# Second MLP product of a hybrid encoder block on one Trainium2 core: its on-chip buffers laid over other buffers of the first product, the residual in two halves, seven stores issued from GpSimd

## The chip, the cores and the metric

The kernel runs on one core of a Trainium2 chip. The metric is the device time of one execution in microseconds; 1725.57 us is the median of three runs of the kernel before, which lay between 1724.66 and 1726.45 us. TensorE (PE), VectorE (DVE), ScalarE (ACT), GpSimd (POOL) and SyncE (SP) each work through an instruction list of their own, in order, and wait for each other on semaphores. An instruction that waits holds up everything behind it on its engine. Transfers are issued by SP, ACT or POOL and then run on 16 DMA engines.

## The reference, cut to what matters

One layer of an encoder block on 1024 tokens of width 1024, in float32. The change lies in the last line.

```python
def hybrid_layer(x, ...):
    h = rmsnorm(x, norm_mix_w)
    proj = h @ w_in
    ...                                   # SSD mixer and neighbourhood attention
    x = x + jnp.concatenate([y_ssm, y_na], axis=-1) @ w_out
    h = rmsnorm(x, norm_mlp_w)
    return x + jnp.square(jax.nn.relu(h @ w_mlp_in)) @ w_mlp_out   # 1024 -> 4096 -> 1024
```

## The kernel before, in words

**Arithmetic.** A float32 product is made of three matmuls on split factors: every factor is cut into a high part and a remainder, and `chain` adds high x high, high x low and low x high. For the second MLP product, the cut costs an ACT pass (`wh` or the high half of `ahl`, line 759) and a subtraction (line 760), which DVE does for activations (the low half of `ahl`) and POOL for weights (`wl`). Both MLP products also use a scheme of seven block products in the place of eight, always in the order `ORD` = 1, 2, 6, 5, 7, 3, 4; its factors are sums and differences of quarter blocks.

**First MLP product** (class `Block`, eight blocks `fb` of 512 hidden columns). The turned and split activations are the factors `hc[1]` to `hc[7]`, two tiles of 8 KB per partition for each, which stay on chip for all eight blocks. They are called h1 to h7 below. One of its seven products is 24 matmuls. `sums` gathers the results of a block in the tiles `cq`: c11 is complete after product 2, c22 after 7, c12 after 3, c21 after 4. ACT squares them, DVE forms the sums s1, s2, s4 and a difference (lines 1203 to 1211), and `store` writes all seven to DRAM as `act_dr`, from the SP queue.

**Second MLP product** (four blocks `fb`, each over 1024 hidden rows as two halves `u`). One of its seven products is 48 matmuls. Its activations come back from `act_dr` into `ar` (line 1272) and are split into `ahl`. Its weight quarters 11, 21, 12 and 22 (line 1289, tiles `wraw`) are split as they are for 1, 2 and 7, and give t1 = 12 - 11, t2 = 22 - t1, 22 - 12 and 21 - t2 on DVE (lines 1306 to 1310) for the others. `acc` is the residual, loaded from `x2_dr`; the block products are added to it from PSUM (line 1330). The last block stores it to the output.

**What lies where.** The pools of the second product are opened after the first has ended, in the same memory. A tile that covers an old one may not be written before the last reader of the old one is done. In the kernel before, counted along the right-hand side, `acc` (32 KB) covers h6 and h5, the split weights `wy` cover raw weights of the first product, the four `ar` buffers cover h4, and the split activations a1, a3, a2 and the raw weights `ra` cover h7, h3, h2 and h1. Eight raw weight buffers `rb` lie on the left, over the four `cq` tiles. `ORD` ends with product 4, so h4 is the last factor to be read.

**What sets the order.** The order of the instructions on each engine is fixed when the program is built, by a scheduler that models times; a wait that is met earlier or later on the chip does not change it. `tc.issue_after` holds an instruction behind another.

Of the kernel before, what the change touches and what calls it, by code (L numbers as in the profile page):

```python
# [9 lines left out]
F32 = mybir.dt.float32  # L10
# [8 lines left out]
P = 128  # L19
T = 1024  # L20
D = 1024
NT = T // P
# [33 lines left out]
def hymba_block(  # L56
# [1039 lines left out]
    with ExitStack() as ph:  # L1096
# [13 lines left out]
        class Block:  # L1110
# [62 lines left out]
                self.s = sA[:, 0], sA[:, 1], sB[:, 0]  # L1173

            def store(self, i, src):
                nc.sync.dma_start(
                    act_dr[self.fb // 2][i - 1, :, 2 * (self.fb % 2) : 2 * (self.fb % 2) + 2, :],
                    src,
                )
# [68 lines left out]
    with ExitStack() as ph:  # L1248
        phase["ps"] = ph.enter_context(
            tc.tile_pool(name="ps4", bufs=1, space=PSUM, reuse_waits="tile")  # L1250
        )
        xa, wy, ar_, a1, a3, a2, ra = (
            ph.enter_context(tc.tile_pool(name=n, bufs=1, side="right", reuse_waits="tile"))
            for n in ("xa", "wy", "ar", "a1", "a3", "a2", "ra")
        )
        rb = ph.enter_context(tc.tile_pool(name="rb", bufs=1, reuse_waits="tile"))
        acc = xa.tile([P, NT, D], F32, name="acc")
        hls[:] = [wy] * 3 + [wp] * 3
        ring["hl"] = ring["raw"] = 0
        raw_a = [wp] * 2 + [ra] * 4  # L1260
# [9 lines left out]
        def a_split(fb, i, u):  # L1270
            ar = ar_.tile([P, 1024], F32, tag="ar", name="ar", bufs=4)
            nc.sync.dma_start(
                ar.rearrange("p (a t) -> p a t", a=2), act_dr[fb][i - 1, :, 2 * u : 2 * u + 2, :]
            )
            pool = ahl[ring["ahl"] % 6]
            ring["ahl"] += 1
            t = pool.tile([P, 2, 1024], F32R, tag="ahl", name="ahl", bufs=2)
            split_to((t[:, 0], t[:, 1]), ar, nc.vector)
            return t[:, 0], t[:, 1]

        for fb in range(4):
            bq = []
            for u in range(2):
                bq.append({n: raw_of(n) for n in ("11", "21", "12", "22")})
            for n in ("11", "21", "12", "22"):
                for u in range(2):
                    r0 = (2 * fb + u) * 512 + (int(n[0]) - 1) * 256
                    d0 = (int(n[1]) - 1) * 512
                    nc.sync.dma_start(
                        bq[u][n].rearrange("p (a d) -> p a d", a=2),  # L1290
                        w_mlp_out[0][r0 : r0 + 256, d0 : d0 + 512].rearrange(
                            "(a p) d -> p a d", p=P
                        ),
                    )
            X = [ps_mm("px2") for _ in range(4)]
            Y = [ps_tp("py2"), ps_tp("py2"), ps_s("py2"), ps_s("py2")]
            if fb == 0:
                for t in range(NT):
                    nc.sync.dma_start(acc[:, t, :], x2_dr[t])
            for i in ORD:  # L1300
                wa = []
                for u in range(2):
                    q = bq[u]
                    if i == 6:
                        q["t1"], q["t2"] = raw_of("t1"), raw_of("t2")
                        nc.vector.tensor_tensor(q["t1"], q["12"], q["11"], op=sub)
                        nc.vector.tensor_tensor(q["t2"], q["22"], q["t1"], op=sub)
                        nc.vector.tensor_tensor(q["12"], q["22"], q["12"], op=sub)
                    elif i == 4:
                        nc.vector.tensor_tensor(q["21"], q["21"], q["t2"], op=sub)  # L1310
                    src = q[{1: "11", 2: "21", 3: "22", 4: "21", 5: "t1", 6: "t2", 7: "12"}[i]]
                    wa.append((a_split(fb, i, u), w_split(src, nc.gpsimd)))
                if i == 5:
                    Y = [ps_tp("pz2"), ps_tp("pz2"), ps_s("pz2"), ps_s("pz2")]
                for t in range(4):
                    pt = (X if i in (1, 6, 7, 4) else Y)[t]
                    ts = slice(t * P, t * P + P)
                    for u in range(2):
                        (ah, al), (wh, wl) = wa[u]
                        for a in range(2):  # L1320
# [8 lines left out]
                    d = acc[:, tt, dh * 512 : (dh + 1) * 512]  # L1329
                    nc.vector.tensor_tensor(d, d, pt, op=add)  # L1330
# [46 lines left out]
```

## Time and profile before

| | |
|---|---|
| median of 3 runs | 1725.57 us |
| the profiled execution's own time | 1725.33 us |
| its span in the trace | 1723.5 us |
| busy, PE / DVE / ACT / POOL | 1636.0 / 1106.3 / 726.5 / 705.6 us |
| last matmul of the first MLP product ends | 1389.7 us |
| first matmul of the second MLP product | 1399.64 us |
| last matmul of the program | 1719.33 us |

The profile gives 1.8 us less for the span than the execution took. A row of the timeline shows the start, the duration, the engine, the source line, the operation, the tile written and the tile read, with the number of instructions that were merged; in brackets stand the idle time of the engine ahead of it and what ended it. PE busy is 95% of the span, yet the few waits that PE has late in the program stand in its row of waits, and the granted clock is listed for each stretch.

### The profile page before, as it was taken

Reading aid. Unit: us, or ns where it says so; the run is one execution under the profiler, and the core shown is the slowest. Engines: PE = TensorE matmul, PEld = TensorE weight load, DVE = VectorE, ACT = ScalarE, POOL = GpSimd, SP = SyncE. Lnnn points to the kernel's source line nnn. Section 1 sums busy time; section 2 is a strip of 40 time slices with the busy share of each in tenths; the row PEclk is TensorE's granted clock in tenths of the full one; section 3 lists DMA queues with packets and bytes.
Section 4 is the critical chain, followed back from the end, with each engine's and each line's share of the span. In section 5 each row is a group of like instructions: output and inputs, shape, how many; then the busy total and the mean of one; then the engine's idle time right before and its main releaser. Section 6 shows DMA issues by size and latency. Waiting matters only on the chain. (4 is left out here: it accounts for less than half of the span.)

```text
span 1723.5 us, 20879 instructions
## 1 busy us (share of the span) xinstructions
PE 1636.0 (95%) x7461; PEld 1304.6 (76%) x7461; DVE 1106.3 (64%) x1687; ACT 726.5 (42%) x1189; POOL 705.6 (41%) x496
## 2 busy tenths in 40 slices
PE   6999999989888999999999988999999978999999
PEld 5788888777766777777767767788888866888887
DVE  5767214889787744778787776454343359787863
ACT  5434223434344434555565533454444443333330
POOL 4000004888778741221242242244444426555551
PEclk9999999999998999999999999999999989999999
DMA  8213338876675796754453141254344394644231
GB/s 200 62 37 104 89 98 242 210 195 207 213 206 161 234 311 199 240 150 138 132 183 123 56 159 49 73 190 153 134 159 147 125 349 149 201 141 166 92 110 73
DMA packets 178499, 269.75 MB, mean 157 GB/s; under 512 B 13963, under 2 KB 105051, under 8 KB 178395
## 3 DMA queue, kind: packets, MB, share of 16 engines
q1 hardware_dynamic: 135419, 231.18, 42.6%
q10 hardware_dynamic: 42976, 37.23, 7.1%
q8 instruction: 59, 0.97, 0.2%
q14 instruction: 45, 0.37, 0.1%
HBM read 185.21 MB, written 86.50 MB: 158 GB/s over the span
## 5 line engine op out<-in xcount | busy, mean ns | idle before, releaser
L760 POOL TENSOR_TENSOR wl<-wraw,wh 128x1024 fp32r<-128x1024 f32 x110 | 300.1, 2740 | 350.1 <-ACT wh L759 336.7
L745 PE MATMUL px<-wh,ahl 128*128 128x512 f32 x512 | 163.7, 397 | 9.8 <-ACT ahl L759 9.8
L759 ACT ACTIVATE wh<-wraw 128x1024 fp32r<-128x1024 f32 x110 | 115.7, 1054 | 127.4 <-issue 42.4
L179 PE MATMUL pq<-wl,hTh 128*128 128x512 f32 x384 | 153.1, 400 | 4.6 <-DVE wl L149 4.4
L745 PE MATMUL px<-h,wh 128*128 128x512 f32 x496 | 156.5, 396 | 0.0
L178 PE MATMUL pq<-wh,hTh 128*128 128x512 f32 x384 | 153.1, 401 | 1.9 <-ACT wh L148 1.2
L180 PE MATMUL pq<-wh,hTl 128*128 128x512 f32 x384 | 151.9, 396 | 0.0
L759 ACT ACTIVATE ahl<-ar 128x1024 fp32r<-128x1024 f32 x56 | 58.9, 1053 | 173.0 <-PE px L745 89.6
L760 DVE TENSOR_TENSOR ahl<-ar,ahl 128x1024 fp32r<-128x1024 f32 x56 | 107.3, 1917 | 37.4 <-ACT ahl L759 36.2
L745 PEld LDWEIGHTS px<-wh,ahl 128*128 128x128 f32 x512 | 97.3, 190 | 31.9 <-ACT ahl L759 10.2
L745 PEld LDWEIGHTS px<-h,wh 128*128 128x128 f32 x496 | 93.4, 189 | 22.4
L149 DVE TENSOR_TENSOR wl<-wraw,wh 128x1024 fp32r<-128x1024 f32 x40 | 55.0, 1376 | 83.3 <-ACT wh L148 82.7
L878 POOL TENSOR_TENSOR mb<-braw,nam 128x256 f32<-128x256 f32 (+1 forms) x48 | 41.0, 884 | 159.7 <-DVE nmx L936 123.4
L184 ACT ACTIVATE pth<-ptp 128x384 fp32r<-128x384 f32 (+1 forms) x128 | 58.4, 459 | 107.8 <-PE ptp L959 106.8
L745 PE MATMUL px<-wl,ahl 128*128 128x512 f32 x256 | 100.9, 394 | 0.0
L745 PE MATMUL px<-h,wl 128*128 128x512 f32 x248 | 98.1, 396 | 0.0
L179 PEld LDWEIGHTS pq<-wl,hTh 128*128 128x128 f32 x384 | 73.2, 191 | 22.1 <-DVE wl L149 7.9
L149 POOL TENSOR_TENSOR wl<-wraw,wh 128x1024 fp32r<-128x1024 f32 x18 | 43.8, 2446 | 110.5 <-ACT wh L148 84.3
L745 PE MATMUL pz<-wh,ahl 128*128 128x512 f32 x256 | 82.8, 400 | 6.5 <-DVE acc L1330 5.0
L178 PEld LDWEIGHTS pq<-wh,hTh 128*128 128x128 f32 x384 | 72.9, 190 | 18.2 <-ACT wh L148 2.5
L180 PEld LDWEIGHTS pq<-wh,hTl 128*128 128x128 f32 x384 | 73.2, 191 | 14.7
L612 POOL TENSOR_TENSOR rb<-rb,c 128x512 f32<-128x512 f32 x64 | 75.0, 1192 | 21.5 <-DMA rb<-cum_dr 18.7
(265 smaller groups left out, 4242.6 us busy)
## 6 DMA issues: line engine op xcount, KB each, us to landing
act_dr<-cq SPq DMA_DIRECT2D x56, 512.0 KB, 3.0
ar<-act_dr SPq DMA_DIRECT2D x56, 512.0 KB, 3.8
wraw<-in_w_in_dram SPq DMA_DIRECT2D x44, 512.0 KB, 4.0
rb<-cum_dr SPq DMA_DIRECT2D x32, 512.0 KB, 7.6
wraw<-in_w_mlp_in_dram SPq DMA_DIRECT2D x32, 512.0 KB, 4.7
wraw<-in_w_mlp_out_dram SPq DMA_DIRECT2D x32, 512.0 KB, 5.3
q_dr<-hl ACTq DMA_DIRECT2D x64, 128.0 KB, 3.2
k_dr<-hl ACTq DMA_DIRECT2D x16, 512.0 KB, 3.2
```

Of the source, the lines that this page charges most:

```text
L149: lo_eng.tensor_tensor(lo[:, 0:n], raw[:, 0:n], hi[:, 0:n].bitcast(F32), op=sub)
L178: nc.tensor.matmul(pt, lhsT=ah, rhs=bh, start=first, stop=False)
L179: nc.tensor.matmul(pt, lhsT=ah, rhs=bl, start=False, stop=False)
L180: return nc.tensor.matmul(pt, lhsT=al, rhs=bh, start=False, stop=last)
L184: nc.scalar.activation(hi, src, AF.Copy)
L612: nc.gpsimd.tensor_tensor(rb[:, d], rb[:, d], c1[:, d, c, h0 : h0 + 4].unsqueeze(2).broadcast_to([P, 4, P]), op=sub,)
L745: nc.tensor.matmul(pt, lhsT=a, rhs=b, start=f, stop=l, skip_group_check=True)
L759: nc.scalar.activation(hl[0], src, AF.Copy)
L760: eng.tensor_tensor(hl[1], src, hl[0].bitcast(F32), op=sub)
L878: nc.gpsimd.tensor_tensor(mb[:, s].rearrange("p (s r c) -> p s r c", r=16, c=8), v[:, a:b], nam[:, s].rearrange("p (s r c) -> p s r c", r= ...
```

## The change

1. **Pools.** On the right, from the outer end: `rb` (raw weights 12, 22, t1, t2) over h6 and h5, `wy` as before, x0 (the first half of the residual) over h4, `ra` over h7, a2 over h3, a1 over h2, `ar` over h1. On the left, x1 (the second half of the residual) lies over the `cq` tiles of c21, c22 and s4, and a3 over those of c11, c12, s1 and s2. The rings of the pools keep their sizes.
2. **Residual.** `acc` is two tiles of 16 KB, loaded in the first block behind the factors of product 1 and of product 6. In block 1, `issue_after` holds the raw weights behind the second half's load.
3. **Loads of activations** are taken out of `a_split`; those of products 1 and 2 are issued with the raw weights.
4. **22 - 12** is formed for product 7 in the place of product 6, and in the source both halves' quarters are allocated quarter by quarter.
5. **Stores** of the last block of the first product go out from POOL.

```diff
             def store(self, i, src):
-                nc.sync.dma_start(
+                (nc.gpsimd if self.fb == 7 else nc.sync).dma_start(
...
-        xa, wy, ar_, a1, a3, a2, ra = (
+        rb, wy, x0, ra, a2, a1, ar_ = (
             ph.enter_context(tc.tile_pool(name=n, bufs=1, side="right", reuse_waits="tile"))
-            for n in ("xa", "wy", "ar", "a1", "a3", "a2", "ra")
+            for n in ("rb", "wy", "x0", "ra", "a2", "a1", "ar")
         )
-        rb = ph.enter_context(tc.tile_pool(name="rb", bufs=1, reuse_waits="tile"))
-        acc = xa.tile([P, NT, D], F32, name="acc")
+        x1, a3 = (
+            ph.enter_context(tc.tile_pool(name=n, bufs=1, reuse_waits="tile")) for n in ("x1", "a3")
+        )
+        acc = [p.tile([P, NT // 2, D], F32, name="acc") for p in (x0, x1)]
...
+            first = {}
+            with ExitStack() as order:
+                if fb == 1:
+                    order.enter_context(tc.issue_after(begun.ins))
+                for n in ("11", "21", "12", "22"):
+                    for u in range(2):
...
+                    if n in ("11", "21"):
+                        i = 1 if n == "11" else 2
+                        first[i] = [a_load(fb, i, u) for u in range(2)]
...
-            if fb == 0:
-                for t in range(NT):
-                    nc.sync.dma_start(acc[:, t, :], x2_dr[t])
...
+                    elif i == 7:
                         nc.vector.tensor_tensor(q["12"], q["22"], q["12"], op=sub)
...
-                    wa.append((a_split(fb, i, u), w_split(src, nc.gpsimd)))
+                    ar = first[i][u] if i in first else a_load(fb, i, u)
+                    wa.append((a_split(ar), w_split(src, nc.gpsimd)))
+                if fb == 0 and i in (1, 6):
+                    h = i == 6
+                    for t in range(4):
+                        begun = nc.sync.dma_start(acc[h][:, t, :], x2_dr[4 * h + t])
```

The change moves instructions on every engine. Three places matter: what SP loads at the seam, what POOL and DVE do there, and where ACT takes up the second product.

On SP, at the seam between the two products, before: the stores of the last block (`act_dr3`) and the first loads of activations stand among each other, and the eight loads of `acc` stand just ahead of this piece. PE among the waits means a wait for a matmul, here the last reader of what the tile covers.

```order
L1176 DMA act_dr3_5437<-cq_11121 128x1024 [waits DMAHW1_49,DVE_49,Activation_49]
L1176 DMA act_dr3_5437<-cq_11122 128x1024 [waits DMAHW2_49,DVE_49]
L1289 DMA wraw_11399<-in_w_mlp_out_dram 128x2x512 [waits DMAHW3_49]
L1176 DMA act_dr3_5437<-cq_11122 128x1024 [waits DMAHW4_49,DVE_49]
L1289 DMA wraw_11400<-in_w_mlp_out_dram 128x2x512 [waits DMAHW5_49]
L1272 DMA ar_11427<-act_dr0_5434 128x1024 [waits DMAHW6_49,PE_49]
L1176 DMA act_dr3_5437<-cq_11120 128x1024 [waits DMAHW7_49,DVE_49]
L1176 DMA act_dr3_5437<-cq_11121 128x1024 [waits DMAHW0_49,Activation_49]
L1272 DMA ar_11436<-act_dr0_5434 128x1024 [waits DMAHW1_49]
L1176 DMA act_dr3_5437<-cq_11123 128x1024 [waits DMAHW2_49,DVE_49]
```

The same place on SP now; 11403 to 11406 are the raw quarters 12 and 22, 11401 and 11402 the quarter 21, each for u = 0 and 1.

```order
L1299 DMA wraw_11403<-in_w_mlp_out_dram 128x2x512 [waits DMAHW0_49,PE_49]
L1299 DMA wraw_11404<-in_w_mlp_out_dram 128x2x512 [waits DMAHW1_49,PE_49]
L1299 DMA wraw_11405<-in_w_mlp_out_dram 128x2x512 [waits DMAHW2_49]
L1299 DMA wraw_11406<-in_w_mlp_out_dram 128x2x512 [waits DMAHW3_49]
L1274 DMA ar_11409<-act_dr0_5434 128x1024 [waits DMAHW4_49]
L1274 DMA ar_11411<-act_dr0_5434 128x1024 [waits DMAHW5_49]
L1299 DMA wraw_11401<-in_w_mlp_out_dram 128x2x512 [waits DMAHW6_49,PE_49]
L1299 DMA wraw_11402<-in_w_mlp_out_dram 128x2x512 [waits DMAHW7_49]
L1274 DMA ar_11415<-act_dr0_5434 128x1024 [waits DMAHW0_49]
L1274 DMA ar_11417<-act_dr0_5434 128x1024 [waits DMAHW1_49]
L1328 DMA acc_11397<-x2_dr_5433 128x1024 [waits DMAHW2_49,PE_49]
```

The four waits for PE are now, in this order, for products 6, 5, 7 and 4 of the last block; `ar` needs no wait of its own, since h1 was read before. All stores are gone from here.

On POOL, the difference from the last instructions of the mixer on: 107 weight remainders in a row before, and the seven stores among them now.

```order
-L760 TENSOR_TENSOR wl<-wraw,wh 128x1024 x107
-L1373 UNCONDITIONAL_BRANCH
-L1373 ISA
+L760 TENSOR_TENSOR wl<-wraw,wh 128x1024 x49
+L1176 DMA act_dr_5437<-cq 128x1024
+L760 TENSOR_TENSOR wl<-wraw,wh 128x1024 x4
+L1176 DMA act_dr_5437<-cq 128x1024 x6
+L760 TENSOR_TENSOR wl<-wraw,wh 128x1024 x54
```

The four in the middle are those of products 3 and 4 of the last block and of product 1 of the second MLP product (u = 0, 1); the remainders of its product 2 now stand behind the last store, which waits for DVE's line 1211.

On DVE, the difference in the last block of the first product, whose sums are line 1190 (py, px, pz are the PSUM tiles of products 2, 7 and 3):

```order
 L1190 TENSOR_TENSOR cq<-cq,py_11159 128x512
+L1316 TENSOR_TENSOR wraw<-wraw 128x1024
 L1190 TENSOR_TENSOR cq<-cq,px_11112 128x512
 L1190 TENSOR_TENSOR cq<-cq,px_11113 128x512
+L1317 TENSOR_TENSOR wraw<-wraw 128x1024
+L1316 TENSOR_TENSOR wraw<-wraw 128x1024
+L1319 TENSOR_TENSOR wraw<-wraw 128x1024
 L1190 TENSOR_TENSOR cq<-cq,pz_11228 128x512
+L1317 TENSOR_TENSOR wraw<-wraw 128x1024
+L1319 TENSOR_TENSOR wraw<-wraw 128x1024
 L1190 TENSOR_TENSOR cq<-cq,pz_11229 128x512
```

Six weight differences of the second product moved up among these sums. A little further on, DVE's list now reads as follows; 11431 and 11438 are the activations of product 1, 11501 and 11508 those of product 2.

```order
L1211 TENSOR_TENSOR cq_11123<-cq_11121,cq_11122 128x1024 [waits DMAHW7_49,DVE_49,Activation_49]
L760 TENSOR_TENSOR ahl_11431<-ar_11409,ahl_11431 128x1024 [waits DMAHW4_49,Activation_49]
L760 TENSOR_TENSOR ahl_11438<-ar_11411,ahl_11438 128x1024 [waits DMAHW5_49,Activation_49]
L1321 TENSOR_TENSOR wraw_11401<-wraw_11401,wraw_11568 128x1024 [waits DMAHW6_49,Pool_49]
L760 TENSOR_TENSOR ahl_11501<-ar_11415,ahl_11501 128x1024 [waits DMAHW0_49,Activation_49]
L1321 TENSOR_TENSOR wraw_11402<-wraw_11402,wraw_11581 128x1024 [waits DMAHW7_49,Pool_49]
L760 TENSOR_TENSOR ahl_11508<-ar_11417,ahl_11508 128x1024 [waits DMAHW1_49,Activation_49]
```

The two subtractions 21 - t2 (line 1321), which before stood among the sums of product 2, now stand between the activations of product 2, and each waits for POOL to have read the old value for `wl`.

On ACT, at the end of the last block and the first split of the second product, before:

```order
L1195 ACTIVATE cq_11120<-cq_11120 128x1024
L1196 ACTIVATE cq_11120<-cq_11120 128x1024
L1187 ACTIVATE cq_11121<-px1_11112 128x512
L1187 ACTIVATE cq_11121<-px1_11113 128x512
L1196 ACTIVATE cq_11121<-cq_11121 128x1024
L759 ACTIVATE wh_11441<-wraw_11399 128x1024
L759 ACTIVATE wh_11502<-wraw_11396 128x1024
L759 ACTIVATE wh_11511<-wraw_11400 128x1024
L759 ACTIVATE ahl_11429<-ar_11427 128x1024
```

And now:

```order
L759 ACTIVATE wh_11441<-wraw_11400 128x1024
L1195 ACTIVATE cq_11121<-cq_11121 128x1024
L1196 ACTIVATE cq_11121<-cq_11121 128x1024
L1195 ACTIVATE cq_11120<-cq_11120 128x1024
L1187 ACTIVATE cq_11121<-px1_11112 128x512
L1196 ACTIVATE cq_11120<-cq_11120 128x1024
L1187 ACTIVATE cq_11121<-px1_11113 128x512
L1196 ACTIVATE cq_11121<-cq_11121 128x1024
L759 ACTIVATE ahl_11431<-ar_11409 128x1024
```

Three weight splits left the place ahead of the first activation split, which still stands behind all work on the last block's results.

More of the change, by code (lines that the diff above doesn't have):

```diff
@@ L1268, in raw_of, with a_load @@
             return ring_tile("rb", raw_b, ("wraw",), (F32,))[0]
-        def a_split(fb, i, u):
+        def a_load(fb, i, u):
             ar = ar_.tile([P, 1024], F32, tag="ar", name="ar", bufs=4)
@@ L1274, in a_split @@
             )
+            return ar
+        def a_split(ar):
             pool = ahl[ring["ahl"] % 6]
@@ L1328, in hymba_block @@
                     tt = 4 * th + t
-                    d = acc[:, tt, dh * 512 : (dh + 1) * 512]
+                    d = acc[th][:, t, dh * 512 : (dh + 1) * 512]
                     nc.vector.tensor_tensor(d, d, pt, op=add)
```

23 lines of the change are left out of this document (11 added, 12 removed).

## The prediction

> **What bounds the kernel now.** I read the page first, then PE's row of waits, then the timeline at the seam between the two MLP products, then a table of three stretches of it.
>
> ```profile
> PE 1636.0 (95%) x7461; PEld 1304.6 (76%) x7461; DVE 1106.3 (64%) x1687; ACT 726.5 (42%) x1189; POOL 705.6 (41%) x496
> ```
>
> ```profile
> PE px L745 <- ACT ahl L759: 9.8, 1, 9.8
> PE pz L745 <- DVE acc L1330: 5.0, 1, 5.0
> PE pz L745 <- DVE ahl L760: 1.5, 1, 1.5
> ```
>
> ```profile
> 1389.72:1424.56 34.84, 25.07 (x97) 20.17 (x97) 21.13 (x16) 13.09 (x13) 14.11 (x5) 0.80 0.94 341
> 1424.56:1455.67 31.11, 24.65 (x98) 19.17 (x97) 31.02 (x21) 13.22 (x14) 19.16 (x6) 0.89 0.50 169
> 1455.67:1719.56 263.89, 263.89 (x1153) 216.10 (x1151) 186.43 (x166) 84.77 (x87) 131.65 (x44) 1.00 0.39 131
> ```
>
> PE bounds, and from 1300 us to the end it waits three times only, all in the first block of the second product. The table's columns are the length, the busy time of PE, PEld, DVE, ACT and POOL, the granted clock, the DMA share and GB/s. The third stretch is 24 block products of 48 matmuls without a wait: 263.89 / 24 = 11.0 us for one. The first two hold two products each, 22.0 us at that pace, so they lose 12.8 and 9.1 us: 21.9 us in all, which is the most that the change can bring. Of it, 9.9 + 5.0 + 1.5 us is waiting, and the rest is matmuls at a lower clock (0.80 and 0.89).
>
> ```profile
> 1378.52 0.63 PE L745 MATMUL pz<-h,wh 128*128 128x512 f32 x2
> 1384.12 0.63 PE L745 MATMUL px<-h,wh 128*128 128x512 f32 x2
> 1389.49 0.39 PE L745 MATMUL px<-h,wl 128*128 128x512 f32 x1
> 1399.64 0.79 PE L745 MATMUL px<-wh,ahl 128*128 128x512 f32 x1 [9.77 <-ACT ahl L759]
> 1413.49 0.39 PE L745 MATMUL py<-wh,ahl 128*128 128x512 f32 x1
> 1424.56 1.08 PE L745 MATMUL px<-wh,ahl 128*128 128x512 f32 x4
> 1437.18 0.79 PE L745 MATMUL pz<-wh,ahl 128*128 128x512 f32 x1 [4.97 <-DVE acc L1330]
> ```
>
> A product of the first MLP product takes 5.6 us (1378.52 to 1384.12), so in its last block products 6, 5, 7, 3, 4 end at about 1367.3, 1372.9, 1378.5, 1384.1 and 1389.7. Product 1 of the second one runs from 1399.64 to 1413.49, 13.85 us.
>
> ```profile
> 1390.76 1.21 SPq L1272 DMA_DIRECT2D ar<-act_dr x1
> ```
>
> ```profile
> 1389.91 0.60 ACT L1187 ACTIVATE cq<-px 128x512 f32<-128x512 f32 x1 [2.19 <-PE px L745]
> 1390.54 1.06 ACT L1196 ACTIVATE cq<-cq 128x1024 f32<-128x1024 f32 x1
> 1398.53 1.06 ACT L759 ACTIVATE ahl<-ar 128x1024 fp32r<-128x1024 f32 x1 [0.21 <-DMA ar<-act_dr]
> ```
>
> So the first wait is a load: `ar` covers h4, SP issues it 1 us after product 4, it lands 7 to 8 us later, ACT splits it, PE starts.
>
> **Step 1, `ar` over h1, a1 over h2.** SP now passes its wait for product 5 at 1372.9, and three raw loads and both `ar` of product 1 follow. Even at the 8.2 us of the slowest kind below they land by 1384. The quarter 11 of u = 1 takes the early place that 21 of u = 0 had on SP, so both weight splits of product 1 are made in the last block. What stays ahead of the first split is ACT's own list: the relu and the square of c21, which end at 1390.54 + 1.06 = 1391.6. With 1.06 for the split, PE could start at 1392.7, a wait of 3.0 us.
>
> ```profile
> wraw<-in_w_mlp_out_dram SPq DMA_DIRECT2D x32, 512.0 KB, 5.3
> acc<-x_dr SPq DMA_DIRECT2D x8, 512.0 KB, 8.2
> ```
>
> **Step 2, six weight differences among the last block's sums.** These are DVE's gaps there, and what POOL does to DVE.
>
> ```profile
> 1375.97 0.69 DVE L1190 TENSOR_TENSOR cq<-cq,px 128x512 f32<-128x512 f32 x1 [13.30 <-PE px L745]
> 1378.79 0.69 DVE L1190 TENSOR_TENSOR cq<-cq,px 128x512 f32<-128x512 f32 x1 [2.12 <-PE px L745]
> 1381.52 0.69 DVE L1190 TENSOR_TENSOR cq<-cq,pz 128x512 f32<-128x512 f32 x1 [2.04 <-PE pz L745]
> 1384.32 0.69 DVE L1190 TENSOR_TENSOR cq<-cq,pz 128x512 f32<-128x512 f32 x1 [2.11 <-PE pz L745]
> 1391.63 1.22 DVE L1211 TENSOR_TENSOR cq<-cq 128x1024 f32<-128x1024 f32 x1 [0.78 <-ACT cq L1196]
> ```
>
> ```profile
> 1350.62 1.21 DVE L1205 TENSOR_TENSOR cq<-cq 128x1024 f32<-128x1024 f32 x1
> 1351.76 3.43 DVE L1207 TENSOR_TENSOR cq<-cq 128x1024 f32<-128x1024 f32 x1
> ```
>
> ```profile
> 1351.69 2.41 POOL L760 TENSOR_TENSOR wl<-wraw,wh 128x1024 fp32r<-128x1024 f32 x1 [3.20 <-ACT wh L759]
> 1374.07 4.80 POOL L760 TENSOR_TENSOR wl<-wraw,wh 128x1024 fp32r<-128x1024 f32 x2 [3.19 <-ACT wh L759]
> ```
>
> ```profile
> 1426.36 15.71 POOL L760 TENSOR_TENSOR wl<-wraw,wh 128x1024 fp32r<-128x1024 f32 x5 [2.34 <-ACT wh L759]
> 1429.79 3.44 DVE L1308 TENSOR_TENSOR wraw<-wraw 128x1024 f32<-128x1024 f32 x1
> ```
>
> A DVE subtraction of 128x1024 takes 1.2 us by itself (1350.62), and 3.43 us when POOL's started just before it (1351.69, 2.41 us): they take turns, one whole instruction each, and DVE is done 1.1 us after POOL. With both busy a pair takes about 3.4 us (1429.79; five of POOL's in 15.71). Not all differences fit into the gaps. The first (line 1316) does: its load follows product 6 and lands at 1367.3 + 5.3 = 1372.6, its output covers h5, free at 1372.9, and the next sum comes at 1375.97. Of the other five, three stand ahead of the sum at 1381.52. POOL now has three remainders from 1374.07 to about 1381.3 in the place of two, so they begin to run at 1381.3 and end at 1384.8; that sum ends at 1385.4, two differences at 1387.8, the next sum at 1388.4, 3.4 us later than before. ACT then has c12's relu to 1389.5, half of c21 to 1390.0, c12's square to 1391.1, the other half to 1391.65, c21's square to 1392.7, and the first split to 1393.75. So the first wait is 1393.75 - 1389.7 = 4.0 us, and 3.0 if the differences fit in. DVE's s1, s2, difference and s4 run from 1391.15 to T = 1395.8, against 1392.85 before (1394.2 at the least).
>
> **Step 3, stores from POOL.** No row shows a DMA issued by POOL. Its price is bounded below by SP's issue (0.42 us) and above by a pass of POOL over a tile of that size (2.4 us); I take 1.0, nearer to the issue, since the row of a pass reads and writes all of the data. A price below nothing has no ground, as POOL issued none before.
>
> ```profile
> 1389.74 0.42 SPq L1176 DMA_DIRECT2D act_dr<-cq x1
> ```
>
> The stores of c11 and c22 have room (POOL is idle to 1368 and after 1381.3). The last five become ready from 1392.35 (s1) to T, so POOL is free at 1392.35 + 5 x 1.0 = 1397.3. Only then comes the remainder of the weights of product 2, u = 0. Behind POOL wait DVE's two subtractions 21 - t2, and behind these the low halves of product 2's activations. Taking turns from T on, with DVE's first low half ending at T + 1.2 and 3.4 us for a pair: second low half T + 4.6, 21 - t2 at T + 8.0, product 2's u = 0 at T + 11.4, 21 - t2 at T + 14.8, and, as POOL has then the next remainder ready (its buffer is free when product 1 ends), u = 1 at T + 18.2 = 1414.0; without that one 1411.8.
>
> **Step 4, the low clock after a wait.**
>
> ```profile
> 497.94 0.77 PE L587 MATMUL pcb<-cT,bT 128*128 128x128 f32 x2 [3.12 <-DVE yo L567]
> 500.64 0.63 PE L179 MATMUL pq<-wl,hTh 128*128 128x512 f32 x1
> 501.34 0.39 PE L178 MATMUL pq<-wh,hTh 128*128 128x512 f32 x1
> ```
>
> Product 1 lost 13.85 - 11.0 = 2.9 us to it after 9.8 us of idling; after 3.12 us of idling (497.94) seven matmuls still stand 0.43 us apart in the place of 0.23, 1.4 us. I take 2.2 us after each wait, the middle. The Trainium skill (TensorE: Matmul & The Clock Gate, Part 1) puts the drop at an idle window of about 3.4 us; by that a wait of 3.0 us would cost no clock. The row at 497.94 fell at less, so I keep 2.2.
>
> **The sum.** PE starts at 1393.75 and ends product 1 at 1393.75 + 11.0 + 2.2 = 1406.95. Product 2 runs 8 matmuls (1.8 us) and then needs the low half of u = 1 at 1408.8: it waits to 1414.0, 5.2 us, and ends after its other 40 matmuls (9.2 us) and 2.2 us of low clock at 1425.4. That is 0.8 us later than before (1424.56). The next two products then take 22.0 us and not 31.1: their waits came from DVE, busy 31.02 of 31.11 us there, with six weight differences that are done by now, and line 1330's sums now precede the low halves. In all 9.1 - 0.8 = 8.3 us. The residual hides: its first half is issued at 1389.7 and first added behind the low half of 1414, the second is issued behind that low half and first added in product 5, at about 1439, and each lands in about 8.2 us. Product 6's `ar` follow the low halves of T + 1.2 and T + 4.6, land by 1409, and are needed at 1425. The clean third stretch stays, as the rings keep their sizes. The profiled execution took 1725.33 us, 0.24 less than the median of 1725.57; from the median, 1717.3 us.
>
> **The rivals.** *No second wait.* If DVE finishes both low halves of product 1 while POOL still issues stores, and gets its turns ahead of product 6's remainders, the low half of u = 1 comes by 1408.8. Then product 2 ends at 1406.95 + 11.0 = 1417.9, 6.6 us earlier than before, 1 us more with a first wait of 3.0: gain 15.7 to 16.7, 1709 to 1710 us. For it: from T on the chain itself holds 10.8 us of work (two remainders of 2.4, five subtractions of 1.2), which ends at 1406.6. Against it: POOL's list has product 6's remainders right behind.
>
> *The stores hold POOL.* At x us each, POOL is free at 1392.35 + 5x, and u = 1 comes 16.2 us behind that. The gain is gone when product 2 ends at 1433.7, that is u = 1 at 1422.3, x = 2.75. At 4 us each u = 1 comes at 1428.5, and 6 us are lost: 1732 us. For it: no row has such an issue, and even the upper bound of 2.4 leaves 1723.9. Against: DVE's subtractions stop at the second low half and wait for POOL, so the late stores meet an idle DVE. The Trainium skill has a rule for this case: SBUF — State Buffer, "A bandwidth-pool intuition that's wrong (but worth ruling out)", gives a GpSimd-issued DMA 620 ns alone and 3100 ns beside a DVE copy that keeps GpSimd from writing descriptors; at 3.1 us each, by that page's figure, the estimate would be 1727 us. Its "Who interferes with whom" infers that `tensor_tensor`, which is what DVE runs here, does not do this. No run here shows either.
>
> *A later wait.* If `issue_after`, the order of the raw quarters or the two residual halves starve a later block, one wait of 4 us with its 2.2 of low clock leaves 1723.5 us, and one like the 9.8 ends at 1729. Against: the loads stand a block ahead.
>
> **How the numbers follow.** The two-wait case 0.52, no second wait 0.28, stores that hold POOL 0.12 (two thirds of it at 1722 to 1729, one third above), a later wait 0.08. Within 0.2% (3.5 us), about what a measurement of this kernel can tell from no change, means 1722.1 to 1729. The range 1708.5 to 1722.5 takes in the first two cases, with x from 0.4 to 2.1 us; about 0.18 lie outside. Faster 0.81, same 0.13, slower 0.06.
>
> **What would show it.** PE's first wait: 3 to 4 us, ended by ACT's split of `ahl`; a second one inside py, ended by DVE's `ahl`, of about 5 us; no wait of pz for `acc`. SP's `ar` loads from 1374 us on. DMA issues by POOL of about 1 us with the remainder of product 2 starting at about 1397. The prediction is wrong if PE waits in py for POOL, if there is no wait in py, or if a wait appears behind 1456.

## The result, and the profile after

The changed kernel took 1714.74 us (median of 5 runs, 1710.18 to 1717.39); the kernel before took 1726.45 us beside it (5 runs, 1724.66 to 1727.24). The ratio is 0.993, with a 95% interval of 0.9916 to 0.9944. The gain of 11.7 us is 0.7% of the time, small but clear of the interval; 8.3 was forecast, and 1714.7 lies in the range. The profiled execution took 1713.85 us with a span of 1712.1.

The first row of the page, the row of PE's waits from 1300 us on, and three stretches of the timeline (columns as in the prediction):

```profile
PE 1633.4 (95%) x7461; PEld 1304.1 (76%) x7461; DVE 1113.6 (65%) x1687; ACT 726.6 (42%) x1189; POOL 707.9 (41%) x503
```

```profile
PE px L745 <- ACT ahl L759: 3.3, 1, 3.3
PE py L745 <- DVE ahl L760: 3.2, 1, 3.2
PE pz L745 <- DVE ahl L760: 0.8, 1, 0.8
PE px L745 <- DVE ahl L760: 0.7, 1, 0.7
```

```profile
1389.52:1422.37 32.85, 25.58 (x97) 19.79 (x97) 28.74 (x19) 15.18 (x17) 21.83 (x11) 0.90 0.78 281
1422.37:1444.15 21.78, 21.78 (x97) 18.02 (x96) 16.81 (x14) 7.90 (x9) 11.72 (x4) 1.00 0.88 324
1444.15:1707.89 263.74, 262.95 (x1153) 215.99 (x1151) 192.30 (x165) 87.19 (x89) 130.93 (x44) 1.00 0.39 131
```

PE waits 8.1 us in the place of 16.2. The first two block products still take 32.85 us in the place of 22.0, a loss of 10.9; the next two now run at the clean pace (21.78 us, before 31.11), and the other 24 as before (263.74), a new wait of 0.8 us in front of pz included.

PE, DVE, POOL, ACT and SP at the seam, from the timeline:

```profile
1393.00 0.50 PE L745 MATMUL px<-wh,ahl 128*128 128x512 f32 x1 [3.31 <-ACT ahl L759]
1396.40 1.22 PE L745 MATMUL px<-wh,ahl 128*128 128x512 f32 x2 [0.75 <-DVE ahl L760]
1413.03 0.73 PE L745 MATMUL py<-wh,ahl 128*128 128x512 f32 x2 [3.22 <-DVE ahl L760]
```

```profile
1387.22 0.68 DVE L1190 TENSOR_TENSOR cq<-cq,pz 128x512 f32<-128x512 f32 x1
1393.99 1.22 DVE L1211 TENSOR_TENSOR cq<-cq 128x1024 f32<-128x1024 f32 x1
1395.13 4.55 DVE L760 TENSOR_TENSOR ahl<-ar,ahl 128x1024 fp32r<-128x1024 f32 x2
1399.60 3.40 DVE L1321 TENSOR_TENSOR wraw<-wraw 128x1024 f32<-128x1024 f32 x1
1402.92 3.42 DVE L760 TENSOR_TENSOR ahl<-ar,ahl 128x1024 fp32r<-128x1024 f32 x1
1406.26 3.43 DVE L1321 TENSOR_TENSOR wraw<-wraw 128x1024 f32<-128x1024 f32 x1
1409.61 3.37 DVE L760 TENSOR_TENSOR ahl<-ar,ahl 128x1024 fp32r<-128x1024 f32 x1
```

```profile
1394.37 0.53 POOL L1176 DMA_DIRECT2D act_dr<-cq  x1 [0.60 <-DVE cq L1207]
1395.51 0.53 POOL L1176 DMA_DIRECT2D act_dr<-cq  x1 [0.60 <-DVE cq L1211]
1396.06 19.18 POOL L760 TENSOR_TENSOR wl<-wraw,wh 128x1024 fp32r<-128x1024 f32 x6
```

```profile
1374.38 0.98 SPq L1274 DMA_DIRECT2D ar<-act_dr  x2
```

```profile
1391.90 2.00 ACT L759 ACTIVATE ahl<-ar 128x1024 fp32r<-128x1024 f32 x2
```

The picture is the forecast one: `ar` is issued at 1374, ACT's own list ends the first wait, and the second one ends with the low half that follows two pairs of POOL and DVE (four rows of 3.4 us). The wait of 0.75 us in product 1 was not forecast: it ends with the first of the two low halves that start at 1395.13, which is done at 1396.35.

**A sum that closes.** Ahead of the seam PE has the same work in all kernels below, and yet their seams begin anywhere from 1387.0 to 1393.5 us. So I compare the rest: from the end of the last matmul of the first product to the end of the span. From it I take PE's waits over 0.4 us and half of the time that PE runs at the low clock (the granted clock is 0.50 there, and matmuls stand 0.43 us apart in the place of 0.23), both counted behind the seam:

| kernel | rest, us | waits | half of the low clock | remainder |
|---|---|---|---|---|
| before | 333.7 | 16.2 | 5.3 | 312.2 |
| changed | 322.4 | 8.1 | 3.0 | 311.3 |
| ar over h4 | 327.9 | 11.9 | 4.7 | 311.3 |
| stores on SP | 323.2 | 8.0 | 3.7 | 311.5 |
| both of these | 327.6 | 11.4 | 4.6 | 311.6 |
| residual at once | 329.8 | 12.5 | 5.9 | 311.4 |
| six differences late | 329.9 | 13.1 | 5.6 | 311.2 |
| 21 - t2 late | 317.7 | 4.0 | 2.9 | 310.8 |
| seam by hand | 314.5 | 2.2 | 1.7 | 310.6 |
| the same, pz behind px | 312.8 | 1.8 | 0 | 311.0 |

So within about 0.5 us nothing but these waits and the clock behind them tells the variants of the changed kernel apart. The kernel before leaves 0.9 us more: that is the pace of its 24 later products, 263.89 us of PE's time in the third stretch against 262.95 now; why the pace differs stays open. Each row is one profiled execution. In it the gain is 333.7 - 322.4 = 11.3 us: 8.1 of waiting, 2.3 of clock, and 0.9 in the later products.

### The profile page after: what moved, and what is told of

The parts are those of the page before. It is cut to its first block, busy times and chain, and to the rows that moved or that the text cites. A ratio compares the mean times of both kernels' runs of the same rounds, so it can differ in the third digit from the quotient of the medians.

```text
span 1712.1 us, 20899 instructions
## 1 busy us (share of the span) xinstructions
PE 1633.4 (95%) x7461; PEld 1304.1 (76%) x7461; DVE 1113.6 (65%) x1687; ACT 726.6 (42%) x1189; POOL 707.9 (41%) x503
## 5 line engine op out<-in xcount | busy, mean ns | idle before, releaser
L759 ACT ACTIVATE wh<-wraw 128x1024 fp32r<-128x1024 f32 x110 | 115.7, 1055 | 148.6 <-PE px L745 51.5
L760 DVE TENSOR_TENSOR ahl<-ar,ahl 128x1024 fp32r<-128x1024 f32 x56 | 117.7, 2108 | 24.8 <-ACT ahl L759 23.8
L149 DVE TENSOR_TENSOR wl<-wraw,wh 128x1024 fp32r<-128x1024 f32 x40 | 55.4, 1386 | 83.6 <-ACT wh L148 83.0
L148 ACT ACTIVATE wh<-wraw 128x1024 fp32r<-128x1024 f32 x58 | 61.1, 1057 | 49.6 <-PE px L179 18.5
```

The costliest lines, as they stand in the source:

```text
L148: nc.scalar.activation(hi[:, 0:n], raw[:, 0:n], AF.Copy)
L149: lo_eng.tensor_tensor(lo[:, 0:n], raw[:, 0:n], hi[:, 0:n].bitcast(F32), op=sub)
L759: nc.scalar.activation(hl[0], src, AF.Copy)
L760: eng.tensor_tensor(hl[1], src, hl[0].bitcast(F32), op=sub)
```

## Experiments

Ratios are to the kernel before, run on the same chip, each with its 95% interval.

**1. Parts of the change undone.** First `ar` back over h4, with all queues in the same order:

```diff
-        rb, wy, x0, ra, a2, a1, ar_ = (
+        rb, wy, ar_, ra, a2, a1, x0 = (
```

> The changed kernel with one line undone: the pools of ar and of the residual's first half change places, so that ar lies over h4 again, which product 4 of the last block reads last; the order of instructions on all engines stays as in the changed kernel. Theory (the first wait was a load that began with the release of h4): SP can load ar only at about 1390, it lands 7.5 us later, the first wait is 9 to 10 us again in the place of 3.3. The quarters 21 behind it in SP's queue come 10 us later too, so POOL's remainders and DVE's list start some 4 us later: second wait 1 to 2 us, product 2 ends at about 1426, total about 1718 to 1720. Rival (DVE's and POOL's list set the end of product 2, not the first wait): first wait longer, second wait gone, product 2 ends at 1422 to 1423 as in the changed kernel, total 1714 to 1716.

Measured: 1718.93 us, 0.9968 (0.9954 to 0.9983). SP's and ACT's rows:

```profile
1390.32 0.82 SPq L1274 DMA_DIRECT2D ar<-act_dr  x2
```

```profile
1393.43 1.06 ACT L759 ACTIVATE ahl<-ar 128x1024 fp32r<-128x1024 f32 x1 [0.86 <-DMA ar<-act_dr]
```

```profile
1409.73 0.74 PE L745 MATMUL py<-wh,ahl 128*128 128x512 f32 x2 [1.93 <-DVE ahl L760]
1416.34 1.22 PE L745 MATMUL py<-wh,ahl 128*128 128x512 f32 x2 [4.93 <-DVE ahl L760]
```

The total came as the theory said, by another way; of the first wait the theory was wrong. The load is issued as late as before the change, but lands in 3.1 us and not in 7 to 8, so the first wait is 4.2 us and not 9 to 10. Most of what is lost lies in product 2: the quarters 21 stand behind `ar` on SP, POOL's remainders come 4 us later, and its two waits are 6.9 us.

Then the stores back on SP:

```diff
-                (nc.gpsimd if self.fb == 7 else nc.sync).dma_start(
+                nc.sync.dma_start(
```

> The changed kernel with the last block's seven stores issued by SP as before, the rest kept. The scheduler then also moves both subtractions 21 - t2 ahead of both low halves of product 2, and spreads the matmuls of product 2 over its four outputs. Theory of the prediction (the stores cost little on POOL and gain little by being there): SP's loads of ar for product 2 stand behind stores that wait for DVE to about 1395 and land at about 1403; product 2 waits 2 to 4 us, total 1713 to 1717. Rival (taking the stores out of SP's queue is a main part of the gain): the late quarters 21 and ar of product 2 hold up POOL and DVE, product 2 waits 6 us or more and the total is 1719 or above.

Measured: 1714.22 us, 0.9942 (0.9921 to 0.9964), not to be told from the changed kernel; the rest is 323.2 against 322.4 us. Waits of 3.3 and 1.8 us in product 1, and three short ones of about 3 us together from 1446 us on, take the place of the second wait; none comes in product 2, where the theory had it. As long as `ar` of product 1 stands ahead of the late stores on SP, who issues them is worth under 1 us. And both of these undone:

> Both of the last two undone at once: stores issued by SP and ar over h4, all else as in the changed kernel (queues as in the run with stores on SP). With ar over h4 alone the load was issued at 1390.3 and split from 1393.4, 3.1 us later, not 7 to 8 as in the kernel before. Theory (what made the load slow before was what SP had issued just ahead of it and beside it, two raw quarters, a store, another ar and two stores within 3.6 us; here only the other ar, one quarter and two stores follow it): ar lands in 3.5 to 5 us, the first wait is 4.3 to 6 us, total 1717 to 1721. Rival (the release of h4 costs the 8 us whatever stands around it, and the run with ar over h4 alone was lucky): first wait 9 us or more, total above 1722.

Measured: 1718.56 us, 0.9965 (0.995 to 0.998), first wait 4.55 us, as the theory had it. So h4 and SP's stores, even together, do not bring the 9.8 us back: what stood ahead of `ar` in SP's order is still out of the way.

Next the second half of the residual, issued with the first and ahead of product 6's `ar`:

```diff
-            return ar
+            (fb, i) == (0, 6) and behind(got, begun); return ar
...
-                if fb == 0 and i in (1, 6):
-                    h = i == 6
-                    for t in range(4):
-                        begun = nc.sync.dma_start(acc[h][:, t, :], x2_dr[4 * h + t])
+                if fb == 0 and i == 1:
+                    for t in range(8):
+                        h = t // 4
+                        begun = nc.sync.dma_start(acc[h][:, t % 4, :], x2_dr[t])
```

Here `got` is the load of `ar`, and `behind(later, earlier)` adds an edge of issue order.

> The changed kernel with both halves of the residual issued at product 1, and product 6's loads of ar behind all eight on SP; the second half's place is free only when s4 is stored (store issued at 1395.5, 9.1 us to land). Theory (loading the second half late is worth something, as SP's queue stands still until that release): product 6's ar are issued at 1405 to 1407 in the place of 1396 to 1402, the scheduler also puts their low halves behind product 2's last sum, product 6 waits 2 to 4 us, total 1716 to 1719. Rival (product 6's loads have 20 us of room): no wait there, total 1714 to 1715.

Measured: 1721.32 us, 0.9988 (0.9973 to 1.0002); the rest is 329.8 us, 7.4 more than in the changed kernel. SP and PE:

```profile
1387.01 16.80 SPq L1328 DMA_DIRECT2D acc<-x_dr  x8
1403.91 6.72 SPq L1274 DMA_DIRECT2D ar<-act_dr  x4
```

```profile
1424.80 0.50 PE L745 MATMUL px<-wh,ahl 128*128 128x512 f32 x1 [2.15 <-ACT ahl L759]
```

SP needs 16.8 us for the eight loads, 13.3 of them standing in front of the fifth for the place of x1, and product 6 waits 2.15 us, as the theory said. The cost is larger than it gave: product 2's second wait came out at 4.4 us with another stretch of low clock, and the scheduler ordered DVE anew behind it. That the late load is worth something is shown; its size is not, as the two are mixed.

Last the six weight differences, put behind product 2's low halves:

```diff
+                        d6 = nc.vector.tensor_tensor(q["t1"], q["12"], q["11"], op=sub); fb or behind(d6, lows[3][1])
+                        d6 = nc.vector.tensor_tensor(q["t2"], q["22"], q["t1"], op=sub); fb or behind(d6, lows[3][1])
...
+                        d7 = nc.vector.tensor_tensor(q["12"], q["22"], q["12"], op=sub); fb or behind(d7, lows[3][1])
```

Here `lows[3][1]` is the low half of product 2, u = 1.

> The changed kernel with the six weight differences of the first block (lines 1316, 1317 and 1319) put behind product 2's low halves on DVE, so that none stands among the last block's sums; the scheduler then also puts 21 - t2 behind them. Theory of the prediction (step 2: three of them delay the second pz sum by 3 us, but the first wait by 1 us at most, since ACT's list binds anyway; and done early they take work from DVE where it is short): first wait 2.6 to 3.0 us in the place of 3.3, second wait gone, but product 6 then waits 6 to 10 us for its weights, total 1718 to 1723. Rival (the differences are as good late): the waits in products 2 and 6 stay under 2 us together, total about 1711.

Measured: 1721.79 us, 0.9979 (0.9965 to 0.9993). PE's waits:

```profile
PE px L745 <- DVE ahl L760: 7.2, 2, 5.3
PE px L745 <- ACT ahl L759: 2.7, 1, 2.7
PE px L745 <- DVE acc L1346: 2.6, 1, 2.6
```

The first wait falls by 0.6 us only (2.7 against 3.3), the second goes, and 9.8 us of waits for DVE come in products 6 to 7 and later. The scheduler also put 21 - t2 behind the low halves, so two things moved: against the changed kernel the rest is 7.5 us longer (329.9 against 322.4), and against the kernel below with 21 - t2 late 12.2 us (317.7). Standing early, the six differences cost 0.6 us of first wait and save more than ten times that.

**2. Parts of the change alone, in the kernel before.** Three parts, one at a time. First `ar` over h2 (a2 takes h4, the order stays):

```diff
-        xa, wy, ar_, a1, a3, a2, ra = (
+        xa, wy, a2, a1, a3, ar_, ra = (
...
-            for n in ("xa", "wy", "ar", "a1", "a3", "a2", "ra")
+            for n in ("xa", "wy", "a2", "a1", "a3", "ar", "ra")
```

> The kernel before, with one part of the change alone: ar no longer lies over h4; it changes places with a2 (over h2, free since product 2). The order of instructions stays as in the kernel before on all engines. Theory (there ar's loads stand in SP's queue behind a raw quarter and a store at 1389.7 that wait for the end of the last block, so its place in memory sets nothing): first wait 9 to 10 us as before, total 1724 to 1727. Rival (the prediction's reading, that the load waits for the release of h4): ar is issued by 1375 to 1385, the first wait falls to 3 to 4 us, total about 1717 to 1720.

Measured: 1725.02 us, 0.9997 (0.9981 to 1.0013). The first wait is 9.7 us. SP still reaches `ar` only behind a store and a raw quarter:

```profile
1387.34 0.48 SPq L1289 DMA_DIRECT2D wraw<-in_w_mlp_out_dram  x1
1387.87 1.22 SPq L1272 DMA_DIRECT2D ar<-act_dr  x1
```

```profile
1394.37 1.06 ACT L759 ACTIVATE wh<-wraw 128x1024 fp32r<-128x1024 f32 x1 [0.50 <-DMA wraw<-in_w_mlp_out_dram]
1395.63 1.06 ACT L759 ACTIVATE ahl<-ar 128x1024 fp32r<-128x1024 f32 x1 [0.20 <-DMA ar<-act_dr]
```

So in the kernel before the release of h4 was not what PE waited for. ACT's rows show a second limit 0.2 us short of the first: the split of `ar` stands behind the splits of raw quarters, the last of which lands as late. Then the stores from POOL:

```diff
-                nc.sync.dma_start(
+                (nc.gpsimd if self.fb == 7 else nc.sync).dma_start(
```

> The kernel before, with one other part of the change alone: the last block's seven stores issued by POOL. On SP two raw quarters and then all four ar of products 1 and 2 follow the residual's loads directly, with no store between; ar still lies over h4. Theory (what stood ahead of ar and beside it in SP's queue made the load late and slow): ar of product 1 is issued at 1390 and lands in 3 to 5 us, first wait 4.5 to 6.5 us in the place of 9.8; the wait of 5 us for DVE's sums in product 5 stays, since the differences are still made there; total 1719 to 1722. Rival (the release of h4 and the weights' quarters 11 that are loaded late set the first wait): first wait 8 to 10 us, total 1724 to 1727.

Measured: 1732.51 us, 1.0043 (1.0028 to 1.0058): 0.4% slower, which neither theory had. The first wait is 7.4 us, between the two: SP had issued nothing for 11 us ahead of `ar` (from 1379.7 to 1390.92), yet the DMA engines were full (a share of 1.03 in the row), and ACT splits the tile 6.3 us later. And in product 5 PE now stands long for the sums on DVE (line 1330), which the scheduler had put in another order:

```profile
1388.00:1390.90 2.90, 2.89 (x13) 2.00 (x11) 2.63 (x3) 0.73 (x2) 0.53 (x1) 1.00 1.03 398
```

```profile
PE pz L745 <- DVE acc L1330: 11.5, 1, 11.5
```

Last the residual, in one piece, behind product 1's `ar`:

```diff
-            nc.sync.dma_start(
+            got[0] = nc.sync.dma_start(
...
-            if fb == 0:
-                for t in range(NT):
-                    nc.sync.dma_start(acc[:, t, :], x2_dr[t])
...
+                if fb == 0 and i == 1:
+                    with tc.issue_after(got[0].ins):
+                        for t in range(NT):
+                            nc.sync.dma_start(acc[:, t, :], x2_dr[t])
```

> The kernel before, with a third part of the change alone: the residual's eight loads (4 MB) are issued behind product 1's loads of ar, in the place of at 1373. What SP issues ahead of ar (stores and two raw quarters) and ar's place over h4 stay. Theory (in the kernel before the 4 MB keep the DMA queues full from 1374 on, so that ar, issued at 1390.8, took 7 to 8 us in the place of 3): the queues are near empty when ar is issued 1 us behind product 4, it lands in 3.5 to 5 us, the first wait is 5 to 7 us in the place of 9.8. Product 1's sums now stand on DVE ahead of product 2's low halves and wait for the residual, so a new wait in product 2 is likely and the total says little, 1718 to 1730. Rival (SP's stores and raw quarters right ahead of ar hold it up): first wait 9 us or more.

Measured: 1734.09 us, 1.0057 (1.0035 to 1.0079). The theory fell: without the residual's 4 MB the DMA engines were idle until 1382 (the stretch's last columns: share 0.00, 1 GB/s) and again from 1386 to 1388, and the first wait is 9.8 us all the same.

```profile
1374.00:1382.00 8.00, 8.00 (x36) 6.42 (x35) 2.06 (x3) 3.07 (x3) 4.39 (x2) 1.00 0.00 1
```

```profile
1390.29 1.23 SPq L1274 DMA_DIRECT2D ar<-act_dr  x1
```

```profile
1398.10 1.06 ACT L759 ACTIVATE ahl<-ar 128x1024 fp32r<-128x1024 f32 x1 [0.21 <-DMA ar<-act_dr]
```

Here SP issues two raw quarters and a store of 512 KB each within 2 us ahead of `ar`; the DMA engines are then 96% busy, and the load takes 7.8 us (1390.29 to 1398.10) in the place of 3.1. No run took these three away alone. None of the three parts gains alone; of the four undone in the changed kernel three cost 5.5 to 7.5 us of the rest, and the stores 0.8.

**3. What was left in the changed kernel.** The two subtractions 21 - t2 behind product 2's low halves, nothing else moved on any engine:

```diff
-                        nc.vector.tensor_tensor(q["21"], q["21"], q["t2"], op=sub)
+                        d4 = nc.vector.tensor_tensor(q["21"], q["21"], q["t2"], op=sub); fb or behind(d4, lows[3][1])
```

> The changed kernel with one thing moved: in the first block DVE issues its two subtractions 21 - t2 (line 1321) behind both low halves of product 2, in the place of ahead of each; the other queues are the same. Theory (the second wait is the two subtractions that stand in DVE's queue between POOL's remainders and the low halves): low halves of product 2 end at about 1403 and 1406.5, the second wait of 3.2 us goes, product 6 starts at 1418.7 to 1419.2 in the place of 1422.4, total 3 to 3.6 us less than the changed kernel, about 1711.3. Rival (DVE and POOL together are short of time, so the work comes back): a wait of about 3 us appears in product 6 or 5, total unchanged at about 1714.7.

Measured: 1710.66 us, 0.9917 (0.9898 to 0.9936); the interval overlaps that of the changed kernel (0.9916 to 0.9944), so the total alone does not show a gain over it. The trace shows one: the second wait is gone.

```profile
1393.80 11.21 DVE L760 TENSOR_TENSOR ahl<-ar,ahl 128x1024 fp32r<-128x1024 f32 x4
1404.94 6.77 DVE L1321 TENSOR_TENSOR wraw<-wraw 128x1024 f32<-128x1024 f32 x2
```

The rest is 317.7 us, 4.7 less; no wait comes in product 6 or 5. Then the seam by hand, with 21 - t2 late as above:

```diff
+        early = lambda: (behind(late["relu"], lows[1][0]), behind(late["c210"], lows[1][0]), behind(late["c211"], lows[1][0]), behind(late["s1"], lows[1][1]),)
...
-                    wa.append((a_split(ar), w_split(src, nc.gpsimd)))
+                    wa.append((a_split(ar), w_split(src, nc.gpsimd))); len(lows) in (3, 4, 5, 6) and behind(made[1], late["store"]); len(lows) == 4 and [behind(d, lows[3][1]) for d in late["sums"]]; len(lows) == 2 and fb == 0 and early()
```

Here `lows[1]` are the halves of product 1, u = 1 (high, low), `relu` and `c210`, `c211` are ACT's relu of c12 and c21, `made[1]` is a weight remainder of product 2 or 6, `late["store"]` the last store, and `late["sums"]` are product 1's sums.

> The changed kernel with the queues set by hand at the seam: ACT makes both high halves of product 1 ahead of c12's relu, DVE both low halves ahead of s1, the two subtractions 21 - t2 and product 1's sums come behind product 2's low halves on DVE, and POOL keeps its stores ahead of product 2's remainders. Theory (ar for product 1 lands by about 1383 and ACT and DVE are idle there, so the first wait and the low clock behind it are a matter of queue order alone): PE runs through from 1389.5 with no wait, product 2 ends at about 1411.5, product 6's ar (store of s2 at 1393, 9.1 us to land, load 7.5 us) just makes it at 1411 to 1412; total 9 to 10 us less than the changed kernel, about 1705. Rival (product 6's factors go through HBM and cannot come earlier, and DVE and POOL have no time to spare): PE stalls 3 to 6 us at product 6 and the total is 1709 to 1712. A third: the early splits push c12's chain back and the total is unchanged or worse, 1714 to 1718.

Measured: 1705.06 us, 0.9885 (0.9866 to 0.9904). ACT and DVE split product 1 inside the last block of the first product, and PE does not wait at the seam; its only wait is in front of pz:

```profile
1382.26 1.06 ACT L759 ACTIVATE ahl<-ar 128x1024 fp32r<-128x1024 f32 x1 [0.67 <-DMA ar<-act_dr]
```

```profile
1386.88 2.35 DVE L760 TENSOR_TENSOR ahl<-ar,ahl 128x1024 fp32r<-128x1024 f32 x2
```

```profile
PE pz L745 <- POOL wl L760: 2.2, 1, 2.2
```

And with PE's matmuls of product 5 held behind product 6:

```diff
-                    tt = 4 * th + t
+                    tt = 4 * th + t; i == 5 and fb == 0 and [behind(m, late["mm"][-13 - 12 * t]) for m in late["mm"][-12:]]
```

Here `late["mm"]` lists the matmuls as they are written, so the 12 of each output of product 5 come behind the last one of product 6.

> The kernel with the hand-set seam, and PE's matmuls of product 5 (pz) kept behind all of product 6; there the scheduler had put four of them ahead, and PE stood 2.2 us for POOL's remainder of t1 and then ran eight matmuls at the low clock. Theory: that wait and its 1.6 us of low clock go, but product 6's own low halves on DVE (the second ends at 1414) then bind for 1 to 1.5 us: 1.5 to 2.5 us less than with the hand-set seam alone, about 1703. Rival: product 6 has to wait for DVE as long as it did for POOL, no change, 1705.

Measured: 1701.77 us, 0.9871 (0.9852 to 0.989), the fastest of all, with one wait left:

```profile
PE px L745 <- DVE ahl L760: 1.8, 1, 1.8
```

Its interval lies below that of the changed kernel, but overlaps that of the seam by hand; the trace shows the last step as 1.7 us of the rest (314.5 to 312.8). Of the 333.7 us of rest before, 20.8 us are gone; the prediction called 21.9 the most there is.

## Why the prediction was right, and where its terms were off

- **Step 1, `ar` over h1.** The wait came as forecast in kind (ACT's split ends it), 3.3 us for 4.0. The reading behind it, that the first wait was a load that began with the release of h4, was wrong as a cause: moving `ar` alone gains nothing (0.9997), and with `ar` back over h4 in the changed kernel the first wait is 4.2 us, so h4 is worth 0.9 of it. The rest of the 9.8 us came with SP's old order: `ar` stood behind stores that wait for DVE's sums of the last block, and the raw quarters and stores issued with it kept the DMA engines 96% busy from 1390.76 to 1398.5. The sum held because it used the new order, in which `ar` goes out at 1374; that the wrong diagnosis did no harm was luck.
- **Step 2, weight differences.** Its mechanism held. The second pz sum ended at 1387.9 for 1388.4, the first split began at 1391.9 and ended at about 1392.95 for 1393.75, T was 1395.2 for 1395.8. The six cost 0.6 us of first wait, not 1.0.
- **Step 3, POOL's stores.** 0.53 us each for 1.0, so POOL is free at 1396.06 for 1397.3. Even so POOL waits 0.6 us for DVE ahead of each of the last two stores. The pairs of 3.4 us were right (3.40, 3.42, 3.43, 3.37), and the low half of u = 1 ended at 1413.0 for 1414.0. The second wait was mis-sized, 3.2 us for 5.2: 1 us from this low half (0.6 of it from T, 0.4 from the chain behind T), and 1 us because PE came later, at 1409.8 for 1408.8. Product 1 waited 0.75 us for its first low half, a term that the working put at nothing although its own figures give it: T + 1.2 = 1397.0 is behind PE's start and eight matmuls, 1393.75 + 1.8. The working of the rivals puts u = 1 at 16.2 us behind POOL, which gives 1413.5 at a price of 1.0 and not the 1414.0 of the sum.
- **Step 4, the clock.** 2.2 us after each wait was the middle of two rows; it was 3.0 after the first and nothing after the second.
- **The sum.** Product 2 ended at 1422.37 for 1425.4, 2.2 us earlier than before and not 0.8 later. These 3.0 us are the shorter second wait (2.0) and the low clock behind it that did not come (2.2), less 0.9 by which product 1 ended late (1407.83 for 1406.95) and some tenths; that is why more was gained than forecast. The next two products took 21.8 us for 22.0: this term, the bulk of the gain, was right, and with the differences late the waits for DVE came back, as its reason says. One wait of 0.79 us stands at 1459.6. A wait behind 1456 was among the signs of being wrong, so on this point the prediction failed; the cost is small, since the third stretch takes 263.74 us with it and took 263.89 before.
- **The rivals.** *No second wait* lost, for the reason given: remainders of POOL and the two subtractions 21 - t2 stood between; with 21 - t2 out of the way the low halves end in time and the wait is gone. *The stores hold POOL* fell: 0.53 us beside DVE's subtractions (1394.37, while DVE's line 1211 runs from 1393.99) is far from 2.75. The Trainium skill (SBUF — State Buffer, "Who interferes with whom") infers that `tensor_tensor` does not keep GpSimd from writing descriptors; this row agrees. *A later wait* is there with 0.79 us, not with 4.

## What to carry to other kernels

A wait that ends with a load is not yet a wait for the memory the load lies over: read which entries stand ahead of it in its queue, and what the engine that takes the data has in front. Here none of three parts gained alone, while three of the four that were undone in the whole cost 5.5 to 7.5 us: undo one part at a time from the whole rather than trying each alone. Where PE waits for a small split, look whether the engine that makes it was idle a few microseconds earlier: here issue order alone gave another 9.6 us of the rest (322.4 to 312.8; the ratio went from 0.993 to 0.9871).

## What the runs showed of the hardware that was not expected

**The low clock comes in pieces of 3.4 us, and not after each wait.** PE behind the wait of 2.23 us in the seam by hand (rows 0.63 long are at the low clock):

```profile
1413.97 0.63 PE L745 MATMUL px<-wh,ahl 128*128 128x512 f32 x1
1417.37 0.40 PE L745 MATMUL pz<-wh,ahl 128*128 128x512 f32 x1
```

The stretch lasts 3.40 us, which costs 1.7 us; behind the wait of 4.25 us with `ar` over h4 it lasts 3.38. Its ends are not free: in each trace, all changes of the granted clock near the seam lie on one grid of 3.41 us. For the changed kernel, on its grid (the columns are the length, the busy time of PE, PEld, DVE, ACT and POOL, the granted clock, the DMA share and GB/s):

```profile
1390.95:1394.36 3.41, 1.36 (x6) 1.14 (x7) 3.38 (x4) 3.41 (x4) 1.59 (x3) 1.00 0.93 332
1394.36:1397.77 3.41, 2.66 (x7) 1.63 (x6) 3.41 (x3) 3.41 (x5) 2.78 (x3) 0.50 1.01 280
1397.77:1401.18 3.41, 3.41 (x9) 2.64 (x8) 3.41 (x2) 1.81 (x2) 3.41 (x2) 0.50 1.03 420
1401.18:1404.59 3.41, 3.41 (x16) 2.79 (x15) 3.41 (x2) 0.00 (x0) 3.41 (x2) 1.00 1.03 423
1408.01:1411.42 3.41, 1.80 (x8) 1.13 (x7) 3.41 (x2) 2.96 (x3) 3.41 (x2) 1.00 0.25 94
1411.42:1414.83 3.41, 1.80 (x8) 1.50 (x9) 3.41 (x5) 0.00 (x0) 3.41 (x2) 1.00 0.27 76
```

The clock is low in the window behind one with 2.05 us of idling (the first wait), stays low behind one with 0.75, and comes back behind a busy one. The wait of 3.22 us is cut into two windows with 1.6 us each and leaves no low clock. Nor do the waits of 2.72 (six differences late), 1.93 (`ar` over h4) and 1.76 us (pz behind px), none of which puts more than 1.9 us into one window. By these rows the cost of a wait depends on where it falls. This is read from the traces, and no run was made to test it; nor are 2.0 us a general limit, since earlier in the changed kernel's program a window with 1.56 us of idling (564.92 to 568.33) was followed by the low clock. The Trainium skill (TensorE: Matmul & The Clock Gate, Part 1) has a free-running window of 3.4 us, and the grid agrees with it. The Trainium skill gives, in the same place, a whole idle window as the condition; here 2.23 us sufficed.

**The time of a 512 KB load depends on how full the DMA engines are.** SP's loads of `ar` took 3.1 us with nothing under way (`ar` over h4, the row below: share 0.00), 7.8 us behind two quarters and a store just issued, and 6.3 us with the stores on POOL, where SP had issued nothing for 11 us but older transfers kept the engines full. So what counts is all that is still under way, and not only what was issued right ahead.

```profile
1386.00:1390.30 4.30, 4.29 (x19) 3.13 (x17) 2.48 (x3) 1.79 (x3) 0.00 (x0) 1.00 0.00 0
```

The change did not make these loads faster: in the changed kernel they take 6.8 to 8.3 us, but product 1's go out 15 us before the end of the last block.
